# A planner books another fixed part for the time of a split matrix product

## The chip, the cores and the metric

The kernel runs on one core of a Trainium2 chip. The metric is the device time of one execution in microseconds (us). Five engines matter here: TensorE (PE, with its weight loads as PEld), VectorE (DVE), ScalarE (ACT), GpSimd (POOL) and SyncE (SP), which issues the large transfers. Each engine takes its own instructions strictly in the order in which the program wrote them, and waits on semaphores for the others.

## The reference, cut to what matters

Two stacks of two layers each act on one sequence of 256 rows and 1024 columns, all in float32. A layer of the first stack is a mixer (a gated delta rule, a retention and a pooling branch, joined by gates) and a gated feed-forward block. A layer of the second stack is a mixer of three attention branches and a feed-forward block of width 4096.

```python
for l in range(DEPTH):                       # first stack
    x = x + rms_norm(hybrid_mixer(rms_norm(x, ...)), ...)
    x = x + rms_norm(swiglu(rms_norm(x, ...), ...), ...)
for l in range(DEPTH):                       # second stack
    h = h + hybrid_mixer_2(rmsnorm(h, ...), ...)
    h = h + square(relu(rmsnorm(h, ...) @ w_up)) @ w_down
return rmsnorm(h, final_norm)
```

So there are eight phases: mixer, feed-forward, mixer, feed-forward, and the same again for the second stack. Nearly all arithmetic is in products of the 256 rows with large weight matrices. In between stand chains of small dependent steps: the triangular solve and the running state of the delta rule, the retention, the softmaxes of the attention branches, and the norms from one phase to the next.

## The kernel before, in words

**Split products.** A large product is made of three products in a rounded 32-bit form (`fp32r`). ACT makes `hi`, a rounded copy of the weights (`Net.hi`), and DVE makes `lo`, the rest (`Net.lo`). The activations are kept as the same kind of pair. For each block of 128 rows of weights, `unit` and `unit_b` issue three products (hi with hi, lo with hi, hi with lo) with 512 or 256 columns. These are the "split products". `unit` issues them in threes with 512 columns and calls `tick()` after each three; `unit_b` issues six with 256 columns (two times three) and then calls `tick()`.

**Chains.** The small steps are written as generators (`delta`, `retention`, `lane`, `norm_T`, the evacuations of a block). They use plain float32 products (`mm` with float32 operands) and transposes (`tr`). They write tiles named `sd` in PSUM, while most split products write `acc`. A chain's `yield 2` means: go on when what I have issued is done and two of the four `sd` banks are free.

**The planner.** The order in which every engine's instructions are written is made while the program is built. `Net` keeps an estimated time for each engine: `s.clk` is PE's, `V.clk` and `S.clk` are those of DVE and ACT. Each issued operation moves its engine's clock by an estimated cost (`op`). `Engine.cost` has the costs of DVE and ACT, `mm` and `tr` (lines 299 to 313) those of PE. A value is taken to be usable 0.13 us (for a PE reader 0.1 us) after its producer's end, and `s.fin` is the end of what a chain last issued plus that time. At each `tick()`, that is, between groups of split products, the planner first lets `ahead` issue `hi` and `lo` for coming weights, as far as ACT's and DVE's clocks lie within some us of PE's. Then it takes from a heap every chain whose time is not later than `s.clk`, and issues its next operations. `late` holds an operation back whose inputs would not be ready by then, so that it does not block the engine's queue. Nothing else than these estimates says how many split products stand between two steps of a chain.

**What the estimates do not touch.** The list of blocks and their units (`order`) is fixed, and so is the order of the weight transfers (`loads`, issued on SP as earlier weights are used up). The cost of a unit in `work`, which makes the due times, uses its own constant. At the end of each phase, eight pieces of work (`LEAD`) are done for the first 128 rows and then for the second, so that PE has products while the norm between phases is computed.

Of the kernel before, what the change touches and what calls it, by code (L numbers as in the profile page):

```python
# [9 lines left out]
F32 = mybir.dt.float32  # L10
# [105 lines left out]
class Net:  # L116
# [182 lines left out]
    def mm(s, out, l, r, start=True, stop=True):  # L299
        n = r.free_size() if hasattr(r, "free_size") else int(np.prod(r.shape[1:]))  # L300

        def go():
            s.op(s, [l, r], [out], max(n, 128) * 4 / 2400 + 0.004 if l.dtype == F32 else max(n, 64) / 2400 + 0.0018, 0.1)
            s.T.matmul(out, lhsT=l, rhs=r, start=start, stop=stop)  # L304
        s.do(go, s, [l, r], [out])

# [1540 lines left out]
```

## Time and profile before

| | us |
|---|---|
| median of 3 runs | 1878.13 (1877.96 to 1880.21) |
| the profiled execution | 1876.53 |
| its span, first to last instruction | 1874.7 |
| PE busy | 1846.1 (98%) |
| DVE busy | 1302.2 (69%) |
| ACT busy | 1010.6 (54%) |

The span is what the trace covers; the profiled execution's time has 1.8 us more around it. Busy times of PE come from modelled ends of pipelined products (a 256-column product is listed with 0.28 us although the next starts 0.12 us later), so the distance from one start to the next tells more about PE than the length of a product.

### The profile page before, as it was taken

To read this page: it belongs to the slowest core of one execution; us is meant where nothing else is said; L and a number is where in the kernel's file an instruction comes from. 1 tells how busy PE (TensorE), PEld (TensorE's weight loads), DVE (VectorE), ACT (ScalarE), POOL (GpSimd) and SP (SyncE) were. 2 spreads that over 40 slices of the span, in tenths; PEclk is the share of its full clock that TensorE was granted. 3 is DMA by queue.
4 is the path that set the end of the run, shared out by engine and by line. 5 is a ranking of instruction groups with operands and counts; after the bars stand their busy time and mean duration, and the time that the engine had idled before them with its cause. 6 is when DMAs were issued, how large, how long until landed. Compare 5 with 4: busy or idle time off the path is not lost.

```text
span 1874.7 us, 31067 instructions
## 1 busy us (share of the span) xinstructions
PE 1846.1 (98%) x12498; PEld 1668.4 (89%) x12498; DVE 1302.2 (69%) x2544; ACT 1010.6 (54%) x1924; POOL 10.7 (1%) x23
## 2 busy tenths in 40 slices
PE   7999999999999999999999999999999999999998
PEld 6998898999899889989998779988998879998997
DVE  6787768664567887776548987686456897686552
ACT  6744356644566334665445466566554456656551
POOL 0000000000000000000000000000000000000000
PEclk9999999999999999999999999999999999999999
DMA  8542354765255315547544433656553353556640
GB/s 296 197 162 75 98 195 135 270 223 183 72 200 206 130 53 166 198 151 284 188 148 147 148 128 97 214 191 242 207 180 97 135 163 108 180 204 228 209 157 23
DMA packets 144336, 313.52 MB, mean 167 GB/s; under 512 B 5704, under 2 KB 20224, under 8 KB 144064
## 3 DMA queue, kind: packets, MB, share of 16 engines
q1 hardware_dynamic: 143376, 310.08, 48.3%
q0 software_dynamic: 816, 1.46, 0.4%
q8 instruction: 98, 1.61, 0.3%
q14 instruction: 46, 0.38, 0.1%
HBM read 310.47 MB, written 1.05 MB: 166 GB/s over the span
## 4 chain that ended last, share of the span: by engine, by line
PE 91%; DVE 4%; ACT 3%; DMA 1%; issue 1%; SPq 0%; DVEq 0%; ACTq 0%
PE acc L304 59%; PE sd L304 28%; PE sd L311 4%; ACT hi L49 1%; DVE lo L49 1%; DMA raw<-in_w_up_dram 1%; DVE sc L49 0%; DMA raw<-in_ffn_gate_dram 0%; ACT L49 0%; ACT act L49 0%; DMA row<-in_mix_pre_norm_dram 0%; ACT L L49 0%; DVE rsb L49 0%; DVE rqx L49 0%; DVE xn L49 0%
## 5 line engine op out<-in xcount | busy, mean ns | idle before, releaser
L49 DVE TENSOR_TENSOR lo<-raw,hi 128x1024 fp32r<-128x1024 f32 (+3 forms) x703 | 686.7, 1013 | 224.6 <-ACT hi L49 186.2
L49 ACT ACTIVATE hi<-raw 128x1024 fp32r<-128x1024 f32 (+4 forms) x711 | 589.5, 877 | 175.5 <-PE acc L304 58.0
L304 PE MATMUL acc<-hi,xT 128*128 128x512 f32 (+3 forms) x1280 | 395.2, 379 | 2.5 <-ACT hi L49 1.7
L304 PE MATMUL acc<-xT,hi 128*128 128x256 f32 x1920 | 357.0, 287 | 0.0
L304 PE MATMUL sd<-xT,hi 128*128 128x256 f32 x1920 | 346.6, 283 | 0.0
L304 PEld LDWEIGHTS acc<-xT,hi 128*128 128x128 f32 x1920 | 298.5, 191 | 5.8 <-issue 4.2
L304 PEld LDWEIGHTS sd<-xT,hi 128*128 128x128 f32 x1920 | 300.9, 192 | 1.7
L304 PEld LDWEIGHTS acc<-hi,xT 128*128 128x128 f32 x1280 | 234.3, 189 | 45.5 <-issue 2.8
L304 PE MATMUL acc<-hi,actT 128*128 128x512 f32 x864 | 272.4, 390 | 0.0
L304 PE MATMUL sd<-xT,lo 128*128 128x256 f32 x960 | 271.7, 283 | 0.0
L304 PE MATMUL acc<-xT,lo 128*128 128x256 f32 x960 | 271.4, 283 | 0.0
L304 PE MATMUL acc<-lo,xT 128*128 128x512 f32 (+3 forms) x640 | 238.1, 372 | 0.5 <-DVE lo L49 0.5
L304 PEld LDWEIGHTS acc<-hi,actT 128*128 128x128 f32 x864 | 162.3, 188 | 33.3
L304 PEld LDWEIGHTS sd<-xT,lo 128*128 128x128 f32 x960 | 184.2, 192 | 0.0
L304 PEld LDWEIGHTS acc<-xT,lo 128*128 128x128 f32 x960 | 183.6, 191 | 0.0
L304 PE MATMUL acc<-lo,actT 128*128 128x512 f32 x432 | 168.4, 390 | 0.0
L304 PEld LDWEIGHTS acc<-lo,xT 128*128 128x128 f32 x640 | 121.2, 189 | 18.1 <-DVE lo L49 1.5
L304 PE MATMUL acc<-oT,hi 128*128 128x256 f32 x672 | 123.5, 285 | 0.0
L304 PEld LDWEIGHTS acc<-oT,hi 128*128 128x128 f32 x672 | 104.7, 192 | 0.8 <-issue 0.7
L49 DVE SCALAR_TENSOR_TENSOR actT<-actq,actT 128x256 fp32r<-128x256 f32 x84 | 34.2, 424 | 88.2 <-ACT actT L49 87.3
L304 PEld LDWEIGHTS acc<-lo,actT 128*128 128x128 f32 x432 | 81.2, 188 | 15.6
L304 PE MATMUL acc<-oT,lo 128*128 128x256 f32 x336 | 95.0, 283 | 0.0
(332 smaller groups left out, 1920.7 us busy)
## 6 DMA issues: line engine op xcount, KB each, us to landing
raw<-in_w_in_dram SPq DMA_DIRECT2D x110, 1024.0 KB, 5.2
raw<-in_w_up_dram SPq DMA_DIRECT2D x32, 1024.0 KB, 5.8
raw<-in_w_down_dram SPq DMA_DIRECT2D x32, 1024.0 KB, 4.9
raw<-in_ffn_down_dram SPq DMA_DIRECT2D x22, 1024.0 KB, 6.4
raw<-in_ffn_gate_dram SPq DMA_DIRECT2D x20, 1024.0 KB, 5.2
raw<-in_ffn_up_dram SPq DMA_DIRECT2D x20, 1024.0 KB, 5.2
raw<-in_w_out_dram SPq DMA_DIRECT2D x8, 1024.0 KB, 5.0
raw<-in_w_o_dram SPq DMA_DIRECT2D x8, 1024.0 KB, 5.1
```

The lines of the kernel that those rows point to most:

```text
L49: f(*a, **k)
L304: s.T.matmul(out, lhsT=l, rhs=r, start=start, stop=stop)
L311: s.T.transpose(out, a, s.ident if p == 128 else s.ident[0:p, 0:p])
```

## The change

The time that the planner books on PE's clock for a split product has its fixed part changed from 0.0018 to 0.0133 us. A 512-column product is booked with 0.2266 us where it was 0.2151, a 256-column product with 0.1200 where it was 0.1085. The cost of plain float32 products, of transposes and of all other operations stays. No instruction is added, removed or resized by the edit itself; it acts only through the order in which the planner writes them.

```diff
@@ -300,7 +300,7 @@
         n = r.free_size() if hasattr(r, "free_size") else int(np.prod(r.shape[1:]))
 
         def go():
-            s.op(s, [l, r], [out], max(n, 128) * 4 / 2400 + 0.004 if l.dtype == F32 else max(n, 64) / 2400 + 0.0018, 0.1)
+            s.op(s, [l, r], [out], max(n, 128) * 4 / 2400 + 0.004 if l.dtype == F32 else max(n, 64) / 2400 + 0.0133, 0.1)
             s.T.matmul(out, lhsT=l, rhs=r, start=start, stop=stop)
         s.do(go, s, [l, r], [out])
```

## Rows read from the trace of the kernel before

**Rows 1.** The page, its first lines: span, and each engine's busy time.

```profile
span 1874.7 us, 31067 instructions
PE 1846.1 (98%) x12498; PEld 1668.4 (89%) x12498; DVE 1302.2 (69%) x2544; ACT 1010.6 (54%) x1924; POOL 10.7 (1%) x23
```

**Rows 2.** The page, granted TensorE clock in 40 slices of the span, in tenths.

```profile
PEclk9999999999999999999999999999999999999999
```

**Rows 3.** The waits of PE: who waited for whom, us in total, times, longest.

```profile
PE sd L311 <- DVE xn L49: 10.1, 3, 8.1
PE acc L304 <- ACT hi L49: 1.7, 1, 1.7
...
PE sd L311 <- DVE b2d L49: 0.2, 1, 0.2
```

**Rows 4.** The chain that ended last: start us, us, what, and how many.

```profile
361.14 23.03 PE sd L304 x192
...
412.67 10.91 PE acc L304 x48
```

**Rows 5.** PE by groups of one shape: count, busy us, mean ns, idle before.

```profile
L304 PE MATMUL acc<-xT,hi 128*128 128x256 f32 x1920 | 357.0, 287 | 0.0
...
L304 PE MATMUL acc<-hi,xT 128*128 128x512 f32 x1024 | 345.9, 402 | 2.5 <-ACT hi L49 1.7 <-DVE rpa L49 0.8
...
L304 PE MATMUL sd<-Tm,MT 128*128 128x128 f32 x160 | 21.9, 280 | 0.7 <-DVE Tm L49 0.7
...
L304 PE MATMUL acc<-lo,xT 128*128 128x256 f32 x32 | 9.1, 283 | 0.0
```

**Rows 6.** Timeline of PE in a mixer: start us, us, operation, count.

```profile
144.35 1.06 PE L304 MATMUL sd<-Tm,MT 128*128 128x128 f32 x8
145.25 0.60 PE L311 MATMUL sd<-ident,Tm 128*128 128x128 f32 x4
145.60 0.48 PE L304 MATMUL acc<-oT,hi 128*128 128x256 f32 x2
...
146.40 0.40 PE L304 MATMUL acc<-oT,hi 128*128 128x256 f32 x2
...
147.12 1.06 PE L304 MATMUL sd<-B,R 128*128 128x128 f32 x8
```

**Rows 7.** Timeline of ACT in the same stretch.

```profile
145.94 0.60 ACT L49 ACTIVATE R<-sd 128x512 f32<-128x512 f32 x1 [3.54 <-PE sd L311]
```

**Rows 8.** Timeline of DVE in the same stretch.

```profile
145.52 0.68 DVE L49 TENSOR_TENSOR B<-sd,cb 128x512 f32<-128x512 f32 x1
```

**Rows 9.** Timeline of PE between the first mixer and its feed-forward.

```profile
323.25 0.39 PE L304 MATMUL sd<-hi,xT 128*128 128x512 f32 x1
324.62 0.63 PE L311 MATMUL sd<-ident,xn 128*128 128x128 f32 x4 [0.98 <-DVE xn L49]
325.94 0.50 PE L304 MATMUL sd<-hi,xT 128*128 128x512 f32 x1 [0.69 <-ACT xT L49]
```

**Rows 10.** Timeline of ACT just before.

```profile
319.14 0.19 ACT L49 ACTIVATION_READ_ACCUMULATOR nsq<-x 128x1 f32 x1
319.35 1.28 ACT L49 ACT_TABLE_LOAD   x1
320.64 0.60 ACT L49 ACTIVATE act<-sd 128x512 f32<-128x512 f32 x1
321.26 1.28 ACT L49 ACT_TABLE_LOAD   x1
322.55 0.29 ACT L49 ACTIVATE ry<-rv,eps 128x1 f32<-128x1 f32 x1
```

**Rows 11.** Timeline of DVE there.

```profile
319.36 0.16 DVE L49 TENSOR_TENSOR rv<-ns 128x1 f32<-128x1 f32 x1 [0.43 <-ACT nsq L49]
...
323.72 1.42 DVE L49 SCALAR_TENSOR_TENSOR xn<-x,ry,row 128x512 f32<-128x512 f32 x2
```

**Rows 12.** The waits of ACT, the largest on a transfer.

```profile
ACT hi L49 <- DMA raw<-in_w_in_dram: 52.0, 24, 4.3
```

## The prediction

> **What bounds the kernel now.** I read the page's busy lines first. PE is busy 98% of a span of 1874.7 us, DVE 69%, ACT 54% [rows 1], and TensorE's clock is granted at its upper level, 2.4 GHz, in all forty slices [rows 2]. So the question is not who is busy but whether PE ever lacks work. The waits of PE answer it: fifteen kinds of wait, 19.8 us in all when the column is added up, and 8.1 us of that is the single wait before the first norm is there [rows 3]. That leaves 11.7 us of seen idle time in which another order could help. A listed product is longer than the distance to the next, so a wait can hide up to some 0.17 us in a product's modelled tail (0.287 against 0.120 us [rows 4, 5]); the true lost time is somewhat larger than 11.7 us, but not many times so.
>
> Next comes the length of a split product in an undisturbed stretch, from the chain that ended last: 192 products of 256 columns in 23.03 us, which is 0.1199 us each, and 48 of 512 columns in 10.91 us, 0.2273 us each [rows 4]. The planner before books 0.1085 and 0.2151, the new one 0.1200 and 0.2266. The new figures are right to 0.001 us; the old ones were 10% and 5% too small.
>
> **The change part by part.** Nothing is added or removed: 12498 products before and after [rows 1]. This term is 0. Eighteen groups by shape (the first, the largest 512-column one and the last are shown) hold 10368 split products [rows 5]. Their booked time grows by 10368 x 0.0115 = 119 us, on the planner's clock alone; the chip's products take what they took.
>
> What moves is where a chain step is put among the split products. The planner looks at its chains once per group of split products. One such look is six 256-column products, booked 0.651 us before and 0.720 after (0.720 by the trace), or three of 512 columns, 0.645 before and 0.680 after (0.682 by the trace). A step that needs w us from DVE or ACT is put at the first look past w. Before, PE really arrived there 10% or 5% later than booked, so each step had a hidden reserve of that size. The change takes the reserve away. It does not make a chain late; it makes steps stand earlier among the products.
>
> Take one step of the delta rule. PE ends four transposes of Tm, and the next split product starts at 145.60 [rows 6]. ACT copies R from 145.94 to 146.54 [rows 7], while DVE made B from 145.52 to 146.20 [rows 8]. Twelve split products, two looks, stand before the step that uses both, at 147.12 [rows 6]: 0.58 us after R was there. The planner's own sum, from the code: 0.13 + (0.051 + 512/1200) + 0.13 = 0.738 us after the transposes. One look is 0.651 before and 0.720 after, two are 1.30 and 1.44; both planners need two looks. So this step stays, by 0.018 us. A single DVE step costs 0.13 + (0.069 + 512/960) + 0.13 = 0.862 us and also stays at two looks, in both widths. Most regular steps are of these two kinds.
>
> Steps with longer waits can move. With a typical wait of two looks, the booked position shifts by 2 x 0.069 = 0.138 us in 256-column stretches and 2 x 0.0345 = 0.069 us in 512-column ones, which is 19% and 10% of a look. I take 14%. Records that are not split products number 12498 - 10368 = 2130, and a step has four to eight records [rows 6], so I estimate some 300 steps, of which some 40 move by one look. What a moved step costs is bounded from the step above: had it stood after one look it would have been due at 146.40 [rows 6], 0.14 us before R was complete. With some 0.06 us for the signal, an estimate, that is a stall of 0.20 us. At the other end it costs 0, when the planner's estimate holds on the chip. It can even gain where it shortens a chain for which PE waits. Sum for 40 steps: 0 to 8 us. I take 0.04 us each, 1.6 us, because a step moves only if the planner reckons it ready by then, and its estimates lie near the rows (0.74 us booked after the transposes where the rows give 0.94 from 145.60 with the switch of 0.08 us in it, 0.60 booked for B where DVE shows 0.68).
>
> The queues that the order is moved past: on ACT, `hi` waits for weights up to 4.3 us at a time, 52.0 us for the largest kind [rows 12], and any chain step behind it waits too. The planner's transfer time is in us and does not change, so `hi` comes 5 to 10% fewer products after its transfer's issue. PE pays only when a chain or `hi` then arrives late; today that is one wait of 1.7 us [rows 3]. I book 0, with up to 2 us more if that cover is gone. SP's queue keeps its order of weights; the row loads that a timer of 60 us places come some 3 to 6 us earlier in PE's work, far ahead of their use: 0. POOL issues small loads only: 0.
>
> Here the Trainium skill speaks against the change. TensorE: Matmul & The Clock Gate, section "Wait — 56ns, not 53.3ns?", gives a warm product as N / 2.4 GHz plus about 2.5 ns; by it 256 columns would take 109.2 ns, near the old booking, and the new one would place every step too early. The trace disagrees: 119.9 ns over 192 products in a row [rows 4]; this kernel loads new weights for every product. The measurement decides.
>
> The sum is +1.6 us. Against the profiled execution (1876.5, its span 1874.7 and 1.8 around it) this gives 1878.1; that execution lies 1.6 us under the median of the runs, so against the median I forecast 1879.7, say 1880.
>
> **The rivals.** *Slower: single ACT steps fall from two looks to one.* The margin that keeps them is 0.018 us of 0.72 us; any small shift in PE's booked time (a bank that comes free, an ACT queue somewhat ahead) decides. It decides from the point where a step's wait is booked at 0.72 us or less. The price is the 0.20 us above for each, and if 30 of the 300 steps are of this kind (an estimate: the product of Tm alone has 160 records in steps of eight, 20 steps [rows 5, 6]) the total is 6 us, with the 1.6 of the others some 1886 against the median. For it: the reserve really is gone. Against it: the same arithmetic holds a step back as often as it lets it go. Within it I put 1 in 100 for the case that products are in truth shorter than the new booking, against which the stretch speaks [rows 4]; then every step comes early by 0.065 us a look, and 300 steps of two looks would cost up to 39 us, 1917. It is the result that the page named above would give.
>
> *Faster: the norm between mixer and feed-forward is no longer held up.* Here PE runs out of its 48 lead products at 323.5 and waits 0.98 and 0.69 us [rows 9]. The reason is on ACT: after the sums of squares end at 319.33 it loads a table, evacuates a gate, loads the other table back and only then takes the root, at 322.55 [rows 10], although its input was there at 319.52 [rows 11]. The gate's block is 24 products of 512 columns, booked 0.28 us longer now. If this puts the gate behind the root, the root comes 3.0 us earlier, which is more than the wait. The stretch comes once per layer of the first stack (two of the three waits for xn, 2.0 us, are these [rows 3]), so 2 x 1.7 = 3.3 us go, and with one or two of the other small waits some 4 to 6 us: 1873 to 1875. Against it: the shift of 0.28 us is small beside the 1.88 us that the gate's table load and evacuation take, so most likely the gate stays where it is.
>
> *The order hardly changes.* If almost no step crosses a look, the time stays at 1878.
>
> **How the numbers follow.** About 0.2% (3.8 us) is what a measurement of this kernel can tell from no change. I give 42 in 100 to the forecast with the unchanged order in it (its own range 1876 to 1882: same), 31 to slower (the ACT steps, or new late steps at phase ends, beyond +3.8), 27 to faster (the norm, or small waits that the new order happens to miss). The range 1872 to 1889 takes in the faster case, the bound of 8 us for moved steps and 2 us for late `hi`; it leaves out the 1917 and larger accidents.
>
> **What would show it.** Right: the dense stretches keep 0.120 and 0.227 us per product, PE's waits sum to 18 to 24 us, and single ACT and DVE steps still stand two looks after their group. The slower rival shows as many new waits of 0.1 to 0.3 us of `sd` products for ACT tiles in the mixers. The faster one shows ACT taking the root before the gate near 319 us and no wait for xn there. The forecast is wrong if a single stretch gains a wait of several us, or if the waits on PE do not account for the difference in time.

## The result and the profile after

The changed kernel is slower: 1896.94 us median (1893.74 to 1900.04) against 1878.64 (1877.96 to 1880.21), ratio 1.0097 with a 95% interval of 1.0080 to 1.0114, 18.3 us. The profiled execution took 1899.24 us. The first lines of the page, the answer to [rows 1]:

```profile
span 1897.5 us, 31070 instructions
PE 1857.4 (98%) x12498; PEld 1671.1 (88%) x12498; DVE 1306.8 (69%) x2554; ACT 1011.2 (53%) x1915; POOL 10.7 (1%) x23
```

PE has the same 12498 products and no engine has more work worth naming: DVE's `lo` is cut into ten instructions more and ACT's `hi` into seven fewer, and ACT loads two tables fewer. The split products stand in the same order in both kernels; only what stands between them differs. The dense stretches, read from the chain that ended last (start us, us, what, how many), answer to [rows 4] digit for digit:

```profile
354.84 10.91 PE acc L304 x48
365.74 23.03 PE sd L304 x192
```

So neither work nor its speed changed, and the time went into places where PE has nothing to do. The waits of PE (us in total, times, longest), the answer to [rows 3]:

```profile
PE sd L311 <- DVE xn L49: 11.1, 5, 8.6
PE acc L304 <- DVE rpa L49: 4.7, 2, 2.4
PE sd L311 <- DVE rqx L49: 2.4, 4, 0.8
PE sd L304 <- DVE g L49: 2.3, 2, 1.3
```

All the lines of that view add up to 31.5 us where they were 19.8. Three kinds carry 8.6 us of the growth: `rpa` (3.9 more), the last reader of a PSUM bank that the next product needs, `rqx` (2.4) and `g` (2.3). The growth is 11.7 us in all, of a span that grew by 22.8.

The rest shows when the trace is cut up from start to start. I went through PE's records and put each distance between two starts in one of three classes: split products beside each other, at the median distance of their shape (1590.6 us before, 1590.8 after); what is above that median between split products; and everything from the start of the last split product ahead of a float32 step to the start of the second one behind it, less the shares of the two split products in it. The float32 steps with their waits took 261.2 us before and 274.2 after, 13.0 more, in 221 and 223 interruptions. The excess between split products was 5.7 us and is 13.2 at the upper clock, 7.5 more, and 2.7 more at the lower. Ahead of the first product and behind the last 0.6 us went. That makes 22.6 of 22.8.

The lower clock is new. Before, TensorE's granted clock stays at the 2.4 GHz level between 17 us and 1870 us. After, it falls to half four times. In a window that covers this stretch of before, and then in windows around two of the falls (window, us, then PE, PEld, DVE, ACT, POOL busy with counts, granted clock, DMA share, GB/s):

```profile
17.10:1870.40 1853.30, 1839.21 (x12481) 1663.29 (x12479) 1293.52 (x2522) 1000.81 (x1906) 7.69 (x14) 1.00 0.49 166
...
58.72:62.13 3.41, 3.41 (x19) 3.41 (x18) 3.00 (x9) 1.17 (x3) 0.00 (x0) 0.50 0.55 212
...
1041.00:1045.00 4.00, 1.63 (x8) 1.00 (x6) 3.72 (x16) 0.21 (x1) 0.00 (x0) 1.00 0.00 0
1045.20:1048.60 3.40, 3.40 (x16) 2.70 (x16) 2.93 (x7) 1.00 (x4) 0.00 (x0) 0.50 0.00 0
```

The other two are at 823.30 and 1488.90 us. Half the rate over 3.41 us costs up to 1.7 us a time, up to 6.8 in all; part of that stands in the 2.7, the rest among the float32 steps.

By place: I compared when the same numbered split product starts in both traces. At number 1200, in the first mixer, after is 4.5 us behind; its feed-forward adds nothing; at 5550, where the first stack ends, 9.5; in the third mixer it rises to 16.3 (number 6750) and in the fourth to some 24. All of the loss is in the four mixers, where chains meet split products.

**One wait, followed back.** The largest new wait of PE, in the third mixer (start us, us, operation, count, idle before):

```profile
1041.64 0.39 PE L304 MATMUL acc<-hi,xT 128*128 128x512 f32 x1
1044.40 0.47 PE L304 MATMUL acc<-hi,xT 128*128 128x512 f32 x1 [2.37 <-DVE rpa L49]
```

The bank holds 192 columns that DVE evacuates as `b1d` and `rpa`, and in front of them the index key, 64 columns, whose norm is a chain of some fourteen small steps. DVE in the same stretch:

```profile
1029.39 1.23 DVE L49 TENSOR_TENSOR lo<-raw,hi 128x1024 fp32r<-128x1024 f32 x1 [0.41 <-ACT hi L49]
1031.45 1.22 DVE L49 TENSOR_TENSOR lo<-raw,hi 128x1024 fp32r<-128x1024 f32 x1 [0.83 <-ACT hi L49]
1032.59 0.16 DVE L49 TENSOR_SCALAR iw<-acc 128x8 f32<-128x8 f32 x1
...
1037.58 0.16 DVE L49 TENSOR_SCALAR iw<-acc 128x8 f32<-128x8 f32 x1
...
1041.58 0.35 DVE L49 TENSOR_TENSOR b1d<-acc,cb 128x192 f32<-128x192 f32 x1
1041.85 0.34 DVE L49 SCALAR_TENSOR_TENSOR sc<-rl,iw,cb 128x128 f32<-128x128 f32 x1
1042.22 0.81 DVE L49 SCALAR_TENSOR_TENSOR sc<-rl,iw,sc 128x128 f32<-128x128 f32 x2
1042.95 0.48 DVE L49 TENSOR_TENSOR b1d<-acc,cb 128x320 f32<-128x320 f32 x1
1043.35 0.31 DVE L49 TENSOR_TENSOR rpa<-acc,cb 128x160 f32<-128x160 f32 x1
1043.58 0.34 DVE L49 SCALAR_TENSOR_TENSOR sc<-rl,iw,sc 128x128 f32<-128x128 f32 x1
1043.84 0.41 DVE L49 TENSOR_TENSOR rpa<-acc,cb 128x96 f32<-128x96 f32 x2
```

Before, in the same place:

```profile
1018.11 4.84 DVE L49 TENSOR_TENSOR lo<-raw,hi 128x1024 fp32r<-128x1024 f32 x4
1022.86 0.16 DVE L49 TENSOR_SCALAR iw<-acc 128x8 f32<-128x8 f32 x1
...
1024.04 0.16 DVE L49 TENSOR_SCALAR iw<-acc 128x8 f32<-128x8 f32 x1
...
1031.23 0.35 DVE L49 TENSOR_TENSOR b1d<-acc,cb 128x192 f32<-128x192 f32 x1
1031.50 0.41 DVE L49 TENSOR_TENSOR rpa<-acc,cb 128x96 f32<-128x96 f32 x2
```

There four `lo` in a row held DVE until 1022.86, so the chains of both row halves came up together and ran in among each other, the second only 1.18 us behind the first; the last bank was read empty 9.0 us after the first `iw`. After, the `lo` come one by one, the first half's chain gets DVE for itself at 1032.59, the second half's runs behind it from 1037.58, and its bank is free 11.7 us after the first `iw`. PE waited 0.78 us for this bank before and waits 2.37 now, and the clock falls 0.8 us later.

Two things are late here, not one. Before, `rpa` follows 0.27 us after `b1d` (1031.23 to 1031.50); after, it stands 2.26 us behind (1041.58 to 1043.84), because four steps of other work (`sc`) and the evacuation of another block come in between. The same steps stand ahead of the second wait, at 1488.79. One of the runs below tells the two apart: at the constant 0.0145 the halves' chains also start 5.0 us apart, but `rpa` follows within 0.7 us of `b1d`, and PE waits 1.2 us in both places.

### The profile page after: what moved, and what is told of

The parts are those of the page before. It is cut to its first block, busy times and chain, and to the rows that moved or that the text cites. A ratio compares the mean times of both kernels' runs of the same rounds, so it can differ in the third digit from the quotient of the medians.

```text
span 1897.5 us, 31070 instructions
## 1 busy us (share of the span) xinstructions
PE 1857.4 (98%) x12498; PEld 1671.1 (88%) x12498; DVE 1306.8 (69%) x2554; ACT 1011.2 (53%) x1915; POOL 10.7 (1%) x23
## 4 chain that ended last, share of the span: by engine, by line
PE 82%; DVE 11%; ACT 4%; DMA 1%; issue 1%; DVEq 0%; SPq 0%; ACTq 0%
PE acc L304 50%; PE sd L304 28%; PE sd L311 4%; DVE lo L49 2%; DVE L L49 1%; ACT hi L49 1%; DVE mx L49 1%; ACT L L49 1%; DVE sc L49 1%; DMA raw<-in_w_in_dram 1%; DVE rpa L49 0%; DMA raw<-in_ffn_gate_dram 0%; DVE rsb L49 0%; DMA row<-in_mix_pre_norm_dram 0%; ACT nsq L49 0%
## 5 line engine op out<-in xcount | busy, mean ns | idle before, releaser
L49 DVE TENSOR_TENSOR lo<-raw,hi 128x1024 fp32r<-128x1024 f32 (+2 forms) x713 | 689.5, 1001 | 268.2 <-ACT hi L49 217.0
L49 ACT ACTIVATE hi<-raw 128x1024 fp32r<-128x1024 f32 (+2 forms) x704 | 590.7, 884 | 161.5 <-PE acc L304 61.4
L304 PE MATMUL acc<-hi,xT 128*128 128x512 f32 (+3 forms) x1280 | 400.7, 382 | 6.4 <-DVE rpa L49 4.7
L304 PE MATMUL acc<-xT,lo 128*128 128x256 f32 x960 | 272.1, 283 | 0.0
L49 ACT ACTIVATE actq<-sd 128x256 f32<-128x256 f32 x84 | 31.0, 378 | 112.7 <-PE sd L304 112.7
```

The costliest lines, as they stand in the source:

```text
L49: f(*a, **k)
```

## The experiments

The first theory, A: the constant hid a reserve, the planner's other bookings are too short, and the loss grows as the reserve goes. Its rival, B: the order before is a lucky or tuned one, and any other order loses some us whatever the constant's sign. Each run's before was 1878.5 to 1879.4 us on its chip; the ratios are to that. The column F is the float32 steps with their waits by the accounting above, S the excess between split products at the upper clock.

**Other constants.** One number in the line of the change:

```diff
-  ... max(n, 64) / 2400 + 0.0133, 0.1)
+  ... max(n, 64) / 2400 + 0.0030, 0.1)
```

> Only the constant, -0.0060, so a split product is booked 0.0078 us shorter than in the kernel before and the reserve is larger. Theory A: no new waits of PE on chain steps, 1873 to 1882 us. Rival B: a loss as with any other order, 1888 to 1905 us.

> Only the constant, 0.0005. Theory B (any other order loses some 4 to 18 us, and the constant only picks the order): 1882 to 1897 us. Theory A (the loss grows with the constant, since the reserve shrinks): 1877 to 1880 us.

> Only the constant, 0.0030 in place of 0.0018 (0.0133 in the changed kernel). Theory A (the short booking of split products was a reserve for chain steps whose latencies are booked too short): a tenth of the reserve goes, so a tenth of the 18.3 us is lost: 1879 to 1882 us. Rival B (the plan before is a lucky one, and any other order costs about the same): 1888 to 1905 us.

> Only the constant, 0.0075, half way. Theory A: the loss grows with the constant, 1884 to 1892 us. Rival B: no order in it, anywhere from 1885 to 1905 us, not nearer to the kernel before than the changed one is.

> Only the constant, 0.0100. Theory B: 1882 to 1897 us, with no order among the constants. Theory A: between the 1882 us of 0.0075 and the 1897 of 0.0133, some 1887 to 1892.

> Only the constant, 0.0145, a tenth of the step beyond the changed kernel. Theory B: 1882 to 1897 us. Theory A: 1896 to 1901 us.

> Only the constant, 0.0200: the product is booked 0.0067 us longer than it takes, so steps stand too early by about as much as they stood late before. Theory B: 1882 to 1897 us. Theory A: PE now comes before its inputs at many steps, 1903 to 1915 us.

| constant | median us (runs) | ratio, 95% interval | F | S |
|---|---|---|---|---|
| -0.0060 | 1886.97 (4) | 1.0045 (1.0029 to 1.0060) | 267.5 | 8.4 |
| 0.0005 | 1879.54 (8) | 1.0004 (0.9993 to 1.0015) | 262.2 | 7.4 |
| 0.0018, before | 1878.64 | | 261.2 | 5.7 |
| 0.0030 | 1887.55 (4) | 1.0048 (1.0030 to 1.0066) | 264.9 | 12.6 |
| 0.0075 | 1882.36 (10) | 1.0023 (1.0013 to 1.0032) | 264.3 | 8.5 |
| 0.0100 | 1886.89 (4) | 1.0044 (1.0024 to 1.0064) | 267.4 | 8.7 |
| 0.0133, after | 1896.94 | 1.0097 (1.0080 to 1.0114) | 274.2 | 13.2 |
| 0.0145 | 1886.67 (4) | 1.0045 (1.0026 to 1.0065) | 268.8 | 6.3 |
| 0.0200 | 1915.68 (2) | 1.0195 (1.0166 to 1.0225) | 295.2 | 10.1 |

A alone falls. A tenth of the step (0.0030) costs 9 us, half of it some 4, a constant beyond the changed one (0.0145) only 8, and -0.0060, which leaves a larger reserve, costs 8 as well, with F 6.3 us over before. B alone does not hold either: column F rises from 0.0075 on in every row but one and is 295 us at 0.0200, where steps are placed too early by any measure. The waits of PE at 0.0200:

```profile
PE sd L311 <- DVE xn L49: 16.8, 10, 9.2
PE sd L304 <- ACT mx L49: 3.5, 2, 2.8
```

These are waits for chains, as A has them. At 0.0030 most of the extra waiting (5.1 of 6.5 us) is one kind, the bank followed above:

```profile
PE acc L304 <- DVE rpa L49: 5.9, 3, 2.8
```

So there are two parts: a trend from too early steps, a few us up to the changed constant and steep beyond it, and on it a scatter of some 5 us either way from which bank or chain an order happens to hit. The changed constant lies high in that scatter: its neighbours 0.0100 and 0.0145 lose some 8 us each, so some 10 of the 18.3 us belong to this one order and not to the size of the constant. That the trend is one of too early steps is plain only at 0.0200; below it the scatter is as large as the trend.

**Where in the kernel.** The changed constant in one stack only:

```diff
+  max(n, 64) / 2400 + (0.0133 if s.stack == 1 else 0.0018)
```

> The changed constant in the four phases of the first stack alone, the old one in the second. If the losses are local to the steps that moved, the first stack costs what it costs in the changed kernel at product 5550 (9.5 us with two half-clock windows) and the second nothing: 1886 to 1890 us. If the order is coupled throughout: anything from 1879 to 1897.

> The changed constant in the second stack alone. Since the first stack alone cost 1 us, a local loss puts the rest here: 1889 to 1896 us, with the two waits for rpa. If the order is coupled throughout: 1879 to 1888 us.

In the first stack alone: 1880.56 us (9 runs), 1.0009 (0.9999 to 1.0018). In the second alone: 1889.67 (4), 1.0060 (1.0045 to 1.0075). Together some 13 us of the 18; the second stack carries most, and its largest new wait is the bank:

```profile
PE acc L305 <- DVE rpa L49: 4.3, 2, 2.5
```

The missing 5 us, by the profiled executions: at number 5550 the first stack lies 2.8 us better in this run than in after, although PE, ACT and DVE take the same instructions in the same order up to there; this run has no stretch at the lower clock there, where after has two. So these 2.8 us come from the execution and not from the order. Another 1.8 us is regained in the second stack of the first run (6.7 us behind before at number 5550, 4.9 at the end), and the second stack costs 1.6 us less in the second run than in after. The other way counts 1.1 us: by so much the first stack of the second run, in the order of before, was slower than in before.

**Truer bookings.** I noted the planner's own clocks as it wrote each order and compared them, product by product, with the trace. Before, the chip falls behind the booked time steadily, from 2.1 us to 119.7 at product 10200. After, the distance goes from 2.5 to 30.0 and does not grow in dense stretches: the estimate did become true. But against PE the other engines now come late. Weights landed 0.45 us ahead of their booking in the median before, and 0.23 behind it after (1.58 us or more in a tenth of them); DVE's instructions went from 0.10 ahead to 0.12 behind. Three bookings are short by the trace: the time from a producer's booked end to PE's start, the transfer of weights, and `tensor_scalar` with a scalar per row, 0.196 us from start to start for 128 columns against 0.136 booked (0.32 against 0.20 from PSUM). The edits, alone and together:

```diff
+OUT, IN = 0.07, 0.18                      # margin: 0.0, 0.28
-                t = max(t, s.ready.get(k, 0.0) + lat)
+                t = max(t, s.ready.get(k, 0.0) + lat + (OUT if k[0].startswith(("acc_", "sd_")) else 0.0))
...
-            s.ready[k] = s.dmaclk + 0.9
+            s.ready[k] = s.dmaclk + 1.6   # dma; the same in s.fin
...
-                return 0.069 + n / 1920
+                return (0.136 if n > 8 else 0.076) + n / 1920    # honest alone
+            if name == "tensor_scalar" and n > 8:
+                return 0.19 + n / 960
```

`lat` and `margin` use IN for every value that PE reads and OUT for what others read from PSUM, `dma` has the second edit, `honest` has `lat`, `dma` and the third, which was not run alone.

> The changed kernel with the two latencies of PE as the traces show them: a product's result usable by ACT and DVE 0.07 us later than booked, a result of ACT or DVE usable by PE after 0.18 us (0.13 where a step is held back, 0.10 where it is booked). Theory A: the true latencies take the place of the reserve, most of the loss goes: 1876 to 1885 us. Rival B: another order, 1888 to 1905 us. Rival C (the waits come from DVE and ACT queues that are filled up differently, not from latencies): 1890 to 1898 us, with the same long waits for rpa, g and rqx.

> The changed kernel with an explicit reserve: PE may use a result of ACT or DVE 0.28 us after its booked end (0.13 and 0.10 before); the products keep their true time. Theory A2: some of the waits of float32 steps go, 1882 to 1892 us. Rival B: 1882 to 1897 us, with as much time in the float32 steps as the changed kernel (274 us).

> The changed kernel with one more constant: weights are booked to land 0.7 us later (1.6 after the end of the booked transfer, not 0.9), since in the trace of the changed kernel half of them landed over 0.2 us and a quarter over 0.7 us later than booked against PE. Theory A2 (the short booking of PE hid that ACT, DVE and transfers are booked too short; weights are the largest such error): some half of the loss goes, 1884 to 1891 us. Rival B (only the order as such): 1882 to 1897 with the same float32 waits.

> The changed kernel with every booking that the trace shows too short raised: landing of weights by 0.7 us, PE's two latencies to 0.20 and 0.18 us, tensor_scalar by 0.07 to 0.12 us. Theory A2: no reserve is needed any more, 1872 to 1883 us. Rival B: 1882 to 1897 us.

| run | median us (runs) | ratio, 95% interval | F | S |
|---|---|---|---|---|
| lat | 1894.99 (4) | 1.0087 (1.0071 to 1.0103) | 272.1 | 13.0 |
| margin | 1895.55 (3) | 1.0087 (1.0070 to 1.0104) | 269.7 | 14.4 |
| dma | 1897.93 (3) | 1.0101 (1.0084 to 1.0118) | 273.9 | 11.3 |
| honest | 1886.98 (5) | 1.0034 (1.0019 to 1.0048) | 263.1 | 13.2 |

Neither correction alone, nor the explicit reserve, is worth more than 2 us, though F falls with each, by 0.3 to 4.5 us. None of the three reached what theory A or A2 expected of it. `lat` lies in rival C's range, but without C's sign: the waits for `rpa`, `g` and `rqx` shrank from 9.4 to 4.1 us. All together bring F to within 2 us of before and the time down by 10, which is outside A2's range and inside B's. What stays is S, and the wait in it:

```profile
PE sd L314 <- DVE xn L50: 11.3, 5, 9.5
PE acc L307 <- DVE rpa L50: 4.2, 2, 2.8
```

**The bank by itself.** ACT copies the bank's first 264 columns to SBUF ahead of the chain, so the bank is free 0.4 us later and not after the chain:

```diff
         def ev_ik(t, ps):
             ikT = make(t, "ikT", [128, 1, 256])
+            cp = s.ar([128, 264], "ikc")
+            S.activation(cp, ps[:, 0:264], AF.Copy)
+            ps = cp
```

> The changed kernel, with ACT copying the 264 columns of the index key's block to SBUF first, so that the norm's chain on DVE no longer holds the PSUM bank. If PE's wait for rpa (4.7 us in two places) and the half clock behind it (two windows of 3.41 us, about 1.7 us each) are a part of the loss: 1887 to 1892 us, without a wait of PE for rpa. If the loss is the order as such (rival B): 1890 to 1900 us.

> The same edit in the kernel before, whose wait for rpa is 0.8 us. If waits are what counts: 1876 to 1881 us. If any other order costs (rival B): 1882 to 1890 us.

> The kernel with all bookings raised to what the trace shows (1887 us), and the copy of ik_after. If its remaining loss is the wait for rpa (4.2 us) and the half clock behind it (1.7 us): 1879 to 1883 us. Rival B: 1884 to 1895 us.

| the copy in | median us (runs) | ratio, 95% interval | F | S | without it, us |
|---|---|---|---|---|---|
| after | 1887.71 (4) | 1.0051 (1.0036 to 1.0066) | 268.4 | 9.5 | 1896.94 |
| honest | 1880.70 (10) | 1.0014 (1.0005 to 1.0024) | 261.2 | 9.1 | 1886.98 |
| before | 1875.17 (10) | 0.9981 (0.9971 to 0.9990) | 259.2 | 5.6 | 1878.64 |

ACT's copy in after (start us, us, operation):

```profile
1028.66 0.39 ACT L49 ACTIVATE ikc<-acc 128x264 f32<-128x264 f32 x1 [0.31 <-PE acc L304]
...
1030.29 0.36 ACT L49 ACTIVATE ikc<-acc 128x264 f32<-128x264 f32 x1
```

The chains of the halves still stand one behind the other on DVE there:

```profile
1029.53 0.16 DVE L49 TENSOR_SCALAR iw<-ikc 128x8 f32<-128x8 f32 x1
...
1034.06 0.17 DVE L49 TENSOR_SCALAR iw<-ikc 128x8 f32<-128x8 f32 x1
```

But PE no longer waits for them, no `rpa` is left among its waits, and the trace has no stretch at the lower clock between 18 us and 1880. That is what separates the bank from the chain: with the bank free, the serial chains no longer hold PE, and the time is 9.2 us lower. Not all that differs between the two traces is the copy's doing: the first-stack stretches at 58.72 and 823.30 are gone too, where both kernels have the same order. Up to the bank, still in the same order, after is 3.1 us behind the kernel with the copy; 9.1 of the 12.2 us between the two profiled executions come behind that point. After's two waits for `rpa` are 4.7 us, and two half-rate stretches of up to 1.7 us follow them (1045.20 and 1488.90), 8.1 together. The copy in before also beats both kernels, by 3.4 us against before; that is more than was expected, and more than the 0.78 us that PE waited for the bank there, so some of it is order.

With these runs the 18.3 us split as follows, each from a difference of medians: 9.2 the index key's bank (after to after with the copy), 7.0 that come back when the three short bookings are mended (1887.71 to 1880.70; F falls by 7.2 to the 261.2 of before), and 2.1 that remain against before. Each of these differences also holds a change of order, so none is sure to better than that scatter; and which single steps make up the 7.0 stays open.

## Why the prediction was wrong

- *The new figures are right, and nothing is added.* Both held: 0.1199 and 0.2273 us per product, 12498 products.
- *"The change takes the reserve away. It does not make a chain late; it makes steps stand earlier."* The first sentence was the key, and steps do stand earlier. The second sentence's "does not make a chain late" was the misreading: against PE, weights and DVE's instructions came late, by the figures above. A reserve of 5 to 10% lay on everything that the planner books in us, not only on the waits of single chain steps.
- *Single ACT and DVE steps stay at two looks.* Right for the step that I worked out. It still stands two looks behind its transposes, three products of 512 columns and six of 256 (the looks of two blocks are mixed here now), in the answer to [rows 6]:

```profile
143.84 0.60 PE L311 MATMUL sd<-ident,Tm 128*128 128x128 f32 x4
...
145.69 1.05 PE L304 MATMUL sd<-B,R 128*128 128x128 f32 x8
```

- *Some 40 steps moved by one look, 1.6 us (bound 8).* This is the step that failed, in its count and in its price. There are 344 groups of float32 products by kind and place, near the 300 steps that I reckoned, but 293 of them stand earlier among the split products after the change, 18 later and only 33 where they stood; the median of those that moved is 21 products earlier, several looks in place of one. I had reckoned each step from its own wait, as if the one before it stayed. The shifts add up along a chain: in the delta chain of the first mixer they grow from 6 products at its start to 42 at a later product of B and R, and the first step that uses `g` stands 66 earlier. And the price of 0.04 us took the bookings as true, though my own rows had them short: 0.94 us less the 0.08 of the switch against 0.74 booked, and 0.68 against 0.60. The first gap, 0.12 us, is nearly the 0.138 us of reserve that went. F grew by 13.0 us (by an estimate up to 3 of it from the lower clock, at which 6.3 us of these steps ran), and 7.0 us came back when the short bookings were mended with the bank out of the way. It is worst where steps follow each other: four `tensor_scalar` in a row, booked 0.20 each from PSUM, take 1.37 us.

```profile
213.48 1.37 DVE L49 TENSOR_SCALAR rqx<-sd,mv,rr 128x128 f32<-128x128 f32 x4
```

and PE waits twice for `rqx` at the end of their chain, with 2 us of DVE's other work in between:

```profile
218.16 0.66 PE L311 MATMUL sd<-ident,rqx 128*128 128x128 f32 x4 [0.43 <-DVE rqx L49]
219.57 0.63 PE L311 MATMUL sd<-ident,rqx 128*128 128x128 f32 x4 [0.76 <-DVE rqx L49]
```

  With all bookings mended (`honest`) the waits for `rqx` are 0.6 us in place of 2.4.

- *`hi` behind a transfer: 0, up to 2 us if the cover goes.* Booking 0 failed here too. In the first mixer of after ACT waits for weights, and `beta`, 0.19 us of work at the head of the chain of `g`, waits behind:

```profile
42.65 1.06 ACT L49 ACTIVATE hi<-raw 128x1024 fp32r<-128x1024 f32 x1 [2.50 <-DMA raw<-in_w_in_dram]
43.62 0.19 ACT L49 ACTIVATE beta<-ba 128x8 f32<-128x8 f32 x1
```

PE waits at the chain's end, 2.3 us before the clock falls:

```profile
56.46 1.06 PE L304 MATMUL sd<-g,cb 128*128 128x8 f32 x8 [1.31 <-DVE g L49]
```

The kernel with the copy has the same order there, and in its trace ACT's wait for the transfer ends 0.7 us sooner. All of that comes through to PE: its step starts 0.7 us sooner after a wait that is 0.6 us shorter, and the clock does not fall:

```profile
41.94 1.06 ACT L49 ACTIVATE hi<-raw 128x1024 fp32r<-128x1024 f32 x1 [1.76 <-DMA raw<-in_w_in_dram]
...
55.75 1.06 PE L304 MATMUL sd<-g,cb 128*128 128x8 f32 x8 [0.70 <-DVE g L49]
```

So with this order PE pays for a late landing in full. Where the step that uses `g` stands seems to count as well: before, it comes 66 products later and PE does not wait for it, and with all bookings mended ACT waits 2.48 us for the transfer, but `g` is not among PE's waits.
- *What I had not priced at all.* Order on a busy engine. Whether DVE does four `lo` ahead in a row or one at a time sets, in the place followed above, whether two chains run in among each other, and so how long a bank is held. The wait was in sight, 0.8 us for `rpa` in [rows 5]. I did not ask what stands ahead of that reader on DVE; the chain had no slack left there, other steps could come in front of it, and 9.2 us hung on the bank. Nor did I ask what TensorE's clock does after a wait, though [rows 2] showed that it had never fallen: that was a condition of the old time, and four stretches of up to 1.7 us each were the price in the profiled execution.
- *The rivals.* Slower was the right side, given 31 in 100, but at 1886, not 1897, and by single ACT steps that fall from two looks to one, where the runs show whole chains moved and a bank. The faster one did not come: ACT still takes the gate ahead of the root, between two table loads, and PE still waits 0.91 us for `xn` there (0.98 before, [rows 9, 10]):

```profile
323.76 1.28 ACT L49 ACT_TABLE_LOAD   x1
325.06 0.60 ACT L49 ACTIVATE act<-sd 128x512 f32<-128x512 f32 x1
325.67 1.28 ACT L49 ACT_TABLE_LOAD   x1
326.97 0.29 ACT L49 ACTIVATE ry<-rv,eps 128x1 f32<-128x1 f32 x1
```

- *What would show it.* I had set 18 to 24 us for PE's waits; 31.5 refutes the forecast. I had also said that it is wrong if a single stretch gains a wait of several us, and the two banks with their clock do that. The rule of the Trainium skill that I weighed (TensorE: Matmul & The Clock Gate, section "Wait — 56ns, not 53.3ns?", 2.5 ns over N / 2.4 GHz) stays refuted for this kernel: the dense stretches show 13.3 and 14.0 ns over it, and with 13.3 booked the planner's clock kept step with them.

## What to carry to other kernels

An estimate that is wrong on one engine may be the only margin for all the others: before making one booked cost true, compare every booking with the trace, and mend them together. Where a planner's order decides, a tiny change of any number can move the time by the scatter of its orders, here some 5 us either way and once some 10, so judge such a change by several neighbouring values and not by one. Look for the resource that a long chain holds (here a PSUM bank under a norm of fourteen steps): freeing it early by a 0.4 us copy was worth 9.2 us, near the 10.0 of all corrections of the estimates together and far more than any one of them. And in a chain of steps, reckon a shift along the whole chain, not step by step.

## What the hardware showed unexpectedly

The lower clock came after short waits, and not every time. In the profiled run of after, three waits of 0.68, 0.69 and 0.63 us stand between the second mixer and its feed-forward (PE, idle before in brackets), and the clock is at the lower level, 1.2 GHz, from 823.30 to 826.70:

```profile
820.11 0.63 PE L311 MATMUL sd<-ident,xn 128*128 128x128 f32 x4 [0.68 <-DVE xn L49]
821.42 0.51 PE L304 MATMUL sd<-hi,xT 128*128 128x512 f32 x1 [0.69 <-ACT xT L49]
822.77 0.50 PE L304 MATMUL sd<-hi,xT 128*128 128x512 f32 x1 [0.63 <-DVE xT L49]
```

With the constant changed in the first stack only, the order there is the same, the same three waits stand there and the clock did not fall:

```profile
818.29 0.63 PE L312 MATMUL sd<-ident,xn 128*128 128x128 f32 x4 [0.69 <-DVE xn L49]
819.60 0.49 PE L305 MATMUL sd<-hi,xT 128*128 128x512 f32 x1 [0.69 <-ACT xT L49]
820.96 0.51 PE L305 MATMUL sd<-hi,xT 128*128 128x512 f32 x1 [0.62 <-DVE xT L49]
```

So one order can take different times: after's four runs lie 6.3 us apart, and the longer ones have the lower mean clock (1893.74 and 1894.64 us at 0.998 and 0.997 of full speed, 1899.24 and 1900.04 at 0.996 and 0.995). The Trainium skill, TensorE: Matmul & The Clock Gate, section "A second HAM failure mode: psum-queue depth-cycling", tells of a kernel whose matmul groups pause briefly while it cycles through PSUM banks, and whose clock falls and rises for it; the trace agrees in part, with a single wait of 2.37 us for a bank, not many short pauses, ahead of each of the falls at 1045.17 and 1488.90; with the copy that frees the bank both falls are gone, but so are the other two, so the copy alone is not shown to be the reason.
